# Two-layer decoder trunk on one core: smaller first loads kept to four in flight, a shorter warm-up, and a reordered last reduction and store

## The chip, the cores and the metric

The kernel runs on one core of a Trainium2 chip. The metric is the time of one execution on the device in microseconds (us). Three timed runs of the kernel before gave 958.12, 958.21 and 958.51 us, so the median is 958.21. A separate execution was recorded by the hardware profiler; its rows are what this document reads.

Engines are named as in the profile: PE is TensorE's matmuls, PEld its weight loads, DVE is VectorE, ACT is ScalarE, POOL is GpSimd and SP is SyncE. A q behind a name is the engine's instruction queue, which issues DMAs.

## What is computed

The input x is 256 positions by 2048 features, in float32. Two layers follow each other, and a last RMS norm ends the computation:

```python
def _rmsnorm(x, g):
    y = x32 * lax.rsqrt(jnp.mean(x32 * x32, axis=-1, keepdims=True) + NORM_EPS)
    return y * g
# layer 0: h = rmsnorm(x) @ w_in, cut into q, k, v of 8 dilated heads, q, k, v of 4 differential heads, gate z
#          y = concat(dilated mixture, differential attention) * silu(z);  x = x + y @ w_out
# layer 1: h = rmsnorm(x) @ w_in, cut into q, k, v of 16 causal heads, gate z
#          y = attention * silu(z);                                         x = x + y @ w_out
# out = rmsnorm(x, final_norm)
```

Each layer multiplies by 2048 x 8192 input weights and 2048 x 2048 output weights, in float32. So the two layers read 168 MB of weights.

## The kernel before

**Tiling.** The contraction of 2048 is cut into 16 k-tiles of 128. The output columns are cut into chunks: 512 columns wide for v and for the output projection, 256 for q, k and z. Layer 0 begins with a v chunk. In such a chunk each k-tile takes six matmuls of 512 columns, three for each half of the 256 positions.

**Splitting.** Every float32 operand is split into a high part, rounded to the fp32r type, and a low part, the rest. ScalarE makes the high part with a copy (lines 130 and 133), VectorE the low part with a subtraction (131 and 134). A product is then high x high, high x low and low x high (`mm3`, line 310). For x the copy also multiplies by the norm's weight g (`split_x`, lines 162 and 163).

**Loads.** One weight tile `raw` holds four k-tiles of a 512-wide chunk, 1 MB; three of them fit. `load(n)` fetches the tile and `split(m)` splits one half of it, two k-tiles. `split` runs three halves ahead of the matmuls. All loads go through SP's queue in the order in which they are written. The first four tiles (line 95 on) are cut: k-tile 0, k-tile 1, then two at a time, with an x piece of two k-tiles (256 KB) ahead. From tile 4 on a tile is one DMA (line 106).

**Start.** TensorE does ten 128 x 128 float32 matmuls on a constant tile of ones first (line 148; each appears as two passes in the profile). They feed nothing. ScalarE loads its function table meanwhile.

**End.** `last_chunk` does the last 512 columns of the output projection, first for positions 0 to 127, then for 128 to 255 in two pieces of 256 columns. Behind the last matmul VectorE adds the residual (line 471), ScalarE squares the result and accumulates (473), VectorE scales that and adds the sum of the earlier columns (478), GpSimd raises it to the power -0.5 (480). VectorE and ScalarE multiply the four 512-wide pieces by that factor in turn (486, 488), and SP stores them (489).

Of the kernel before, what the change touches and what calls it, by code (L numbers as in the profile page):

```python
# [2 lines left out]

# [5 lines left out]
F32 = mybir.dt.float32  # L9
F32R = mybir.dt.float32r  # L10
AF = mybir.ActivationFunctionType
ALU = mybir.AluOpType
# [3 lines left out]
P = 128  # L16
S = 256
D = 2048
KT = D // P
# [3 lines left out]
SCALE = HD ** -0.5  # L23
LAM_INIT = 0.8 - 0.6 * math.exp(-0.3 * 0)
AHEAD = 3
WARM = 10
RAW_BUFS = 3
SPLIT_BUFS = 4
ALIGN = 512
PAD = 160  # L30
BACK = 224
# [24 lines left out]
def trunk(ctx, tc, x_nat, x_t, w0, o0, w1, o1, g0, g1, gfin, lam, subln, cos_t, sin_t,  # L56
# [30 lines left out]
    def source(n):  # L87
        layer, i = divmod(n, n_layer)
        return (w0, w1)[layer][i] if i < n_in else (o0, o1)[layer][i - n_in]

    def load(n):
        if n >= NR or n in raws:
            return
        t = wpool.tile([P, 4 * CW], F32, tag="raw", name=f"raw{n}", bufs=RAW_BUFS)
        if n == 0:
            for i in range(3):
                if i != 1:
                    load_x(i)
                nc.sync.dma_start(t[:, (0, 1, 2)[i] * CW:(1, 2, 4)[i] * CW],  # L99
                                  source(0)[:, (0, 1, 2)[i] * CW:(1, 2, 4)[i] * CW])  # L100
        elif n < 4:
            for a in (0, 2):
                load_x(4 * n + a)
                nc.sync.dma_start(t[:, a * CW:(a + 2) * CW], source(n)[:, a * CW:(a + 2) * CW])
        else:
            nc.sync.dma_start(t, source(n))
        raws[n] = t
        for f in after_load.get(n, ()):
            f()

    def split(m):
        if m >= 2 * NR:
            return
        load(m // 2)
        r = raws[m // 2][:, 2 * (m % 2) * CW:2 * (m % 2 + 1) * CW]
        last = m - 2 * NR + 8
        if 0 <= last < 4:
            h = [xhl[2 * last + i].rearrange("p a b -> p (a b)") for i in range(2)]
            lo = [xhl[8 + 2 * last + i].rearrange("p a b -> p (a b)") for i in range(2)]
        else:  # L120
            ht = wpool.tile([P, 2 * CW], F32R, tag="wh", name=f"wh{m}")
            lt = wpool.tile([P, 2 * CW], F32R, tag="wl", name=f"wl{m}")
            w = wide[m // 2]
            h, lo = ([t[:, i:i + w] for i in range(0, 2 * CW, w)] for t in (ht, lt))
        if m < 2 or 0 <= last < 4:
            for i in range(2):
                if m == 0:
                    split_x(0, i, xr(i))
                rr = r[:, i * CW:(i + 1) * CW]
                nc.scalar.activation(h[i], rr, AF.Copy)  # L130
                nc.vector.tensor_sub(lo[i], rr, h[i].bitcast(F32))
        else:
            nc.scalar.activation(ht, r, AF.Copy)  # L133
            nc.vector.tensor_sub(lt, r, ht.bitcast(F32))  # L134
        splits[m] = (h, lo)
# [5 lines left out]
    nc.vector.memset(ones, 1.0)  # L141
    nc.vector.memset(half, -0.5)
    warm = small.tile([P, 1], F32, tag="warm", name="warm")
    nc.scalar.activation(warm, half, AF.Tanh)
    xraw = [work.tile([P, 4, S], F32, tag=f"yt{i}", name=f"xraw{i}") for i in range(KT // 4)]
    pw = patt.tile([P, P], F32, tag="O", name="pw")
    for i in range(WARM):
        nc.tensor.matmul(pw, ones, ones, start=True, stop=True)
    def load_x(kt):
        nc.sync.dma_start(xraw[kt // 4][:, kt % 4:kt % 4 + 2], x_t[:, kt:kt + 2])  # L150
        if kt == 0:
            nc.sync.dma_start(g_sb[:, 0], g0)

    def xr(kt):
        return xraw[kt // 4][:, kt % 4]
# [151 lines left out]
                nc.scalar.activation(v, ps[:, tt], AF.Copy, scale=rs)  # L307
        V[layer, g] = (v, vh, vl)

    def mm3(out_, lh, ll, rh, rl, start=True, stop=True):  # L310
        for i, (l, r) in enumerate(((lh, rh), (lh, rl), (ll, rh))):
            nc.tensor.matmul(out_, l, r, start=start and i == 0, stop=stop and i == 2)  # L312

    def softmax(layer, g, h, mask):
        (q, qh, ql), (k, kh, kl) = Q[layer, g], K[layer, g]
# [127 lines left out]
    def last_chunk():  # L443

        base = 2 * NR - 8
        part = small.tile([P, 2], F32, tag="part", name="part")
        fs = small.tile([P, 2, 4], F32, tag="fs", name="fs")
        c0 = 3 * CW
        for tt, widths in ((0, (CW,)), (1, (CW // 2, CW // 2))):
            nc.vector.memset(fs[:, tt], 0.0)  # L450
            at_col = 0
            for i, w in enumerate(widths):
                ps = pacc.tile([P, w], F32, tag="acc", name=f"last{tt}_{i}")
                for kt in range(KT):
                    if tt == 0 and kt % 2 == 0:
                        split(base + kt // 2 + AHEAD)
                    wh, wl = splits[base + kt // 2]
                    cs = slice(at_col, at_col + w)
                    a_h, a_l = yh[kt][:, tt * P:(tt + 1) * P], yl[kt][:, tt * P:(tt + 1) * P]
                    b_h, b_l = wh[kt % 2][:, cs], wl[kt % 2][:, cs]  # L460
                    for j, (l, r) in enumerate(((a_h, b_h), (a_h, b_l), (a_l, b_h))):
                        nc.tensor.matmul(ps, l, r, start=kt == 0 and j == 0, stop=kt == KT - 1 and j == 2)  # L462
                    if tt == 0:
                        for f, a in fill.pop(4 * NR - KT + kt, []):
                            f(*a)
                if i == 0:
                    s = small.tile([P, 1], F32, tag="s1", name="s1", bufs=2)
                    nc.vector.tensor_reduce(s, ssq[:, tt, 0:3], axis=AX.X, op=ALU.add)
                    nc.vector.tensor_scalar(part[:, tt:tt + 1], s, 1.0 / D, EPS, op0=ALU.mult, op1=ALU.add)
# [12 lines left out]
                at_col += w  # L482
            for n in range(4):
                x = x_sb[:, tt, n * CW:(n + 1) * CW]
                if n % 2 == 0:
                    nc.vector.tensor_scalar(x, x, fs[:, tt, 3:4], None, op0=ALU.mult)
                else:
                    nc.scalar.activation(x, x, AF.Copy, scale=fs[:, tt, 3:4])
                nc.sync.dma_start(out[tt * P:(tt + 1) * P, n * CW:(n + 1) * CW], x)


    at(14, first_r_a)
# [12 lines left out]
    for (kind, layer, g, j, w), slot0 in list(zip(chunks, starts))[:-1]:  # L505
# [3 lines left out]
        for slot in range(slot0, nxt):  # L509
            if slot % 2 == 0:  # L510
                split(slot // 2 + AHEAD)
                load((slot // 2 + AHEAD) // 2 + 1)
            if layer == 0 and slot < KT and 2 * AHEAD <= slot + 4 < KT:
                split_x(0, slot + 4, xr(slot + 4))
            wh, wl = splits[slot // 2]
            for i in range(per):
                kt = (slot - slot0) * per + i
                ww = (slot % 2) * per + i
                first, final = kt == 0, kt == KT - 1
                for b in range(2):  # L520
                    bs = slice(b * P, (b + 1) * P)
                    if w == CW:
                        a_h, a_l = (yh[kt][:, bs], yl[kt][:, bs]) if kind == "o" else \
                            (xhl[kt][:, 0, bs], xhl[kt][:, 1, bs])
                        mm3(ps[:, b], a_h, a_l, wh[ww], wl[ww], start=first, stop=final)
# [109 lines left out]
```

## Time and profile before

| | |
|---|---|
| timed runs, median of 3 | 958.21 us (958.12 to 958.51) |
| profiled execution | 958.89 us, of which its span is 957.1 us |
| TensorE busy | 946.3 us, 99% of the span |
| VectorE, ScalarE busy | 639.3 us (67%), 526.3 us (55%) |
| read from HBM, written | 174.15 MB, 2.10 MB |
| mean granted TensorE clock | 0.996 of full speed |

The span runs from the first instruction to the last. A busy share is an average over the whole span. A row of a timeline tells when an instruction started, how long it took and, in brackets, how long its engine had been idle and what ended that. The granted clock is a share of 2.4 GHz, so 0.50 is 1.2 GHz.

### The profile page before, as it was taken

The numbers are of one execution on the slowest core, as the hardware profiler recorded it, in microseconds if no ns is written. First come the engines' busy times: TensorE is split into PE (matmuls) and PEld (weight loads), VectorE is DVE, ScalarE is ACT, GpSimd is POOL, SyncE is SP. The second block draws the span as 40 slices with busy tenths as digits, with TensorE's granted clock in tenths as the row PEclk, the third lists the DMA queues.
The fourth block names the chain that finished last, engine by engine and source line by source line (L and its number), as shares of the span: only waits on it lengthen the run. The fifth ranks groups of instructions, "written<-read, shape, count | busy, mean of one in ns | idle before, by whom it ended". The sixth has DMA issues, their size and how long they took to land.

```text
span 957.1 us, 13108 instructions
## 1 busy us (share of the span) xinstructions
PE 946.3 (99%) x5132; PEld 819.1 (86%) x5132; DVE 639.3 (67%) x973; ACT 526.3 (55%) x807; POOL 6.0 (1%) x12
## 2 busy tenths in 40 slices
PE   8999999999999999999999999999999999999996
PEld 7888888888888888888888898888889888888886
DVE  6778678557856785655566787685678567755572
ACT  7556556445645564454544665564566455644451
POOL 0000000000000000000000000000000000000000
PEclk9999999999999999999999999999999999999999
DMA  9775454445554554544555544545454545554542
GB/s 327 247 295 181 146 190 176 169 175 195 185 173 162 196 179 175 176 176 176 181 176 203 190 169 156 203 155 194 164 191 170 182 173 180 191 205 176 181 171 88
DMA packets 27854, 177.09 MB, mean 185 GB/s; under 512 B 3344, under 2 KB 4112, under 8 KB 7696
## 3 DMA queue, kind: packets, MB, share of 16 engines
q1 hardware_dynamic: 27504, 175.21, 51.5%
q10 hardware_dynamic: 288, 1.05, 0.4%
q8 instruction: 40, 0.66, 0.3%
q14 instruction: 22, 0.18, 0.1%
HBM read 174.15 MB, written 2.10 MB: 184 GB/s over the span
## 4 chain that ended last, share of the span: by engine, by line
PE 96%; issue 1%; DMA 1%; SPq 0%; ACT 0%; DVE 0%; POOL 0%; POOLq 0%; ACTq 0%
PE acc L529 36%; PE acc L312 34%; PE acc L531 19%; PE ps_s L312 1%; PE last L462 1%; PE ps_t L352 1%; DMA raw<-in_w 1%; PE po L312 1%; PE ps_s L317 1%; PE po L383 1%; PE pdo L312 0%; PE ps_xt L426 0%; PE ps_yt L409 0%; SPq L99 0%; SPq L150 0%
## 5 line engine op out<-in xcount | busy, mean ns | idle before, releaser
L134 DVE TENSOR_TENSOR wl<-raw,wh 128x1024 fp32r<-128x1024 f32 x314 | 384.3, 1224 | 244.7 <-ACT wh L133 242.2
L529 PE MATMUL acc<-x,wh 128*128 128x512 f32 x1536 | 541.1, 393 | 0.0
L133 ACT ACTIVATE wh<-raw 128x1024 fp32r<-128x1024 f32 x314 | 332.3, 1059 | 292.5 <-PE acc L529 138.4
L531 PE MATMUL acc<-x,wl 128*128 128x256 f32 x1536 | 432.8, 282 | 0.0
L529 PEld LDWEIGHTS acc<-x,wh 128*128 128x128 f32 x1536 | 288.5, 188 | 58.4
L531 PEld LDWEIGHTS acc<-x,wl 128*128 128x128 f32 x1536 | 290.2, 189 | 0.3
L312 PE MATMUL acc<-wh,x 128*128 128x512 f32 x512 | 164.8, 400 | 1.6 <-ACT wh L130 1.6
L312 PEld LDWEIGHTS acc<-wh,x 128*128 128x128 f32 x512 | 96.9, 189 | 24.8 <-ACT wh L130 1.8
L312 PE MATMUL acc<-wl,x 128*128 128x512 f32 x256 | 101.9, 398 | 0.5 <-DVE wl L134 0.2
L312 PE MATMUL acc<-wh,yh 128*128 128x512 f32 x224 | 88.4, 394 | 0.0
L312 PE MATMUL acc<-wh,yl 128*128 128x512 f32 x224 | 87.3, 390 | 0.0
L312 PE MATMUL acc<-wl,yh 128*128 128x512 f32 x224 | 87.2, 389 | 0.0
L312 PEld LDWEIGHTS acc<-wl,x 128*128 128x128 f32 x256 | 48.5, 190 | 12.6 <-DVE wl L134 0.7
L312 PEld LDWEIGHTS acc<-wh,yl 128*128 128x128 f32 x224 | 42.0, 188 | 9.0
L312 PEld LDWEIGHTS acc<-wl,yh 128*128 128x128 f32 x224 | 42.1, 188 | 8.3
L312 PEld LDWEIGHTS acc<-wh,yh 128*128 128x128 f32 x224 | 42.1, 188 | 8.3
L326 ACT ACTIVATE p<-p,st 128x128 f32<-128x128 f32 x64 | 28.5, 448 | 9.9 <-DVE st L322 9.6
L375 ACT ACTIVATE yh<-y 128x256 fp32r<-128x256 f32 x32 | 13.0, 417 | 34.4 <-DVE y L374 34.3
L290 DVE TENSOR_TENSOR rt<-rt,sr 128x512 f32<-128x512 f32 x32 | 22.1, 690 | 3.7 <-ACT rt L288 2.4
L287 ACT ACTIVATE rt<-rt 64x512 f32<-64x512 f32 x32 | 20.2, 631 | 7.7 <-DVE rt L286 7.0
L286 DVE TENSOR_TENSOR rt<-acc,rt 128x512 f32<-128x512 f32 x32 | 21.8, 683 | 0.1
L288 ACT ACTIVATE rt<-rt 64x512 f32<-64x512 f32 x32 | 20.2, 632 | 0.4
(131 smaller groups left out, 646.9 us busy)
## 6 DMA issues: line engine op xcount, KB each, us to landing
raw<-in_w SPq DMA_DIRECT2D x124, 1024.0 KB, 4.7
raw<-in_o SPq DMA_DIRECT2D x32, 1024.0 KB, 4.7
raw<-in_w SPq DMA_DIRECT2D x7, 512.0 KB, 8.7
xraw<-in_x_t SPq DMA_DIRECT2D x8, 256.0 KB, 7.7
x_sb<-in_x_nat SPq DMA_DIRECT2D x1, 2048.0 KB, 11.0
out<-x_sb SPq DMA_DIRECT2D x8, 256.0 KB, 2.5
gf<-in_gfin ACTq DMA_DIRECT2D x2, 512.0 KB, 4.5
raw<-in_w SPq DMA_DIRECT2D x2, 256.0 KB, 4.5
```

Source lines behind the costliest of these rows:

```text
L133: nc.scalar.activation(ht, r, AF.Copy)
L134: nc.vector.tensor_sub(lt, r, ht.bitcast(F32))
L286: nc.vector.tensor_add(t1, ps[:, :, 0:S], t1)
L287: nc.scalar.activation(t2[0:64], t1[64:128], AF.Copy)
L288: nc.scalar.activation(t2[64:128], t1[0:64], AF.Copy)
L290: nc.vector.tensor_mul(t2, t2, sr[:, None, :].to_broadcast([P, 2, S]))
L312: nc.tensor.matmul(out_, l, r, start=start and i == 0, stop=stop and i == 2)
L317: nc.tensor.matmul(ps[:, 0:P], q[:, h, 0:P], k[:, h, 0:P], start=True, stop=True)
L326: nc.scalar.activation(p[:, sl], p[:, sl], AF.Exp, bias=st[:, 0, i:i + 1], scale=-1.0, accum_out=st[:, 1, i:i + 1])
L375: nc.scalar.activation(yh[kt], y, AF.Copy)
L529: nc.tensor.matmul(ps[:, b], wh[ww][:, bs], xx, start=first, stop=False, skip_group_check=True)
L531: nc.tensor.matmul(ps[:, b, 0:S], wl[ww][:, bs], xx[:, 0:S], start=False, stop=final, skip_group_check=True)
```

## The change

**Loads.** The first four weight tiles and the x pieces with them now go through `fetch`, which makes each load wait until the fourth one before it has landed. The pieces are smaller: k-tile 0 comes in two halves of its columns (128 KB each), k-tiles 1 to 7 one by one (256 KB), k-tiles 8 to 15 in twos as before. x comes as one k-tile (128 KB) with each single weight piece, as two with each double one. The norm's weight g and x of k-tile 0 move from SP's queue to ScalarE's, ahead of its table load.

**Splits and first matmuls.** The copies and subtractions of k-tiles 4 to 7 are done one k-tile at a time (before: two). Those of k-tile 0 are done in two halves of 256 columns, and so are its matmuls: twelve of 256 columns in place of six of 512. The warm-up has five matmuls in place of ten.

**End.** The square, its accumulation and the scaling become one VectorE instruction, a multiply with a running sum that starts at the part known before. The final piece's multiplication by the norm's weight and by the factor become one. The pieces stored are 256 to 512 columns wide and go through both queues: 256, 512, 512 (and for the last positions 256) from VectorE by SP, 256 and the rest from ScalarE by its own queue.

```diff
-WARM = 10
+WARM = 5
...
+IN_FLIGHT = 4
...
+    fetched = []
+
+    def fetch(dst, src):
+
+        i = nc.sync.dma_start(dst, src).ins
+        if len(fetched) >= IN_FLIGHT:
+            tc.add_manual_dep(i, fetched[-IN_FLIGHT].name, mybir.DependencyInfo(
+                mybir.DependencyClass.Sync, mybir.DependencyReason.DATA), reason="loads in turn")
+        fetched.append(i)
...
-        if n == 0:
-            for i in range(3):
-                if i != 1:
-                    load_x(i)
-                nc.sync.dma_start(t[:, (0, 1, 2)[i] * CW:(1, 2, 4)[i] * CW],
-                                  source(0)[:, (0, 1, 2)[i] * CW:(1, 2, 4)[i] * CW])
-        elif n < 4:
-            for a in (0, 2):
-                load_x(4 * n + a)
-                nc.sync.dma_start(t[:, a * CW:(a + 2) * CW], source(n)[:, a * CW:(a + 2) * CW])
+        if n < 4:
+
+            cuts = {0: (0, CW // 2, CW, 2 * CW, 3 * CW, 4 * CW), 1: range(0, 5 * CW, CW)}.get(n, range(0, 5 * CW, 2 * CW))
+            for a, b in zip(cuts, cuts[1:]):
+                if a % CW == 0 and (n or a):
+                    load_x(4 * n + a // CW, max(1, (b - a) // CW))
+                fetch(t[:, a:b], source(n)[:, a:b])
...
-        if m < 2 or 0 <= last < 4:
+        if m < 4 or 0 <= last < 4:
...
-                rr = r[:, i * CW:(i + 1) * CW]
-                nc.scalar.activation(h[i], rr, AF.Copy)
-                nc.vector.tensor_sub(lo[i], rr, h[i].bitcast(F32))
+                n = CW // 2 if m == 0 and i == 0 else CW
+                for a in range(0, CW, n):
+                    rr = r[:, i * CW + a:i * CW + a + n]
+                    nc.scalar.activation(h[i][:, a:a + n], rr, AF.Copy)
+                    nc.vector.tensor_sub(lo[i][:, a:a + n], rr, h[i][:, a:a + n].bitcast(F32))
...
+    nc.scalar.dma_start(g_sb[:, 0], g0)
+    nc.scalar.dma_start(xraw[0][:, 0:1], x_t[:, 0:1])
     nc.scalar.activation(warm, half, AF.Tanh)
...
-    def load_x(kt):
-        nc.sync.dma_start(xraw[kt // 4][:, kt % 4:kt % 4 + 2], x_t[:, kt:kt + 2])
-        if kt == 0:
-            nc.sync.dma_start(g_sb[:, 0], g0)
+    def load_x(kt, n):
+        fetch(xraw[kt // 4][:, kt % 4:kt % 4 + n], x_t[:, kt:kt + n])
...
-                nc.scalar.activation(j, x, AF.Square, accum_out=fs[:, tt, i:i + 1])
-                if i + 1 < len(widths):
-                    nc.vector.tensor_scalar(part[:, tt:tt + 1], fs[:, tt, i:i + 1], 1.0 / D, part[:, tt:tt + 1],
-                                            op0=ALU.mult, op1=ALU.add)
-                else:
-                    nc.vector.tensor_scalar(fs[:, tt, 2:3], fs[:, tt, i:i + 1], 1.0 / D, part[:, tt:tt + 1],
-                                            op0=ALU.mult, op1=ALU.add)
-                    nc.gpsimd.tensor_tensor(fs[:, tt, 3:4], fs[:, tt, 2:3], half, op=ALU.pow)
-                nc.vector.tensor_mul(x, x, gf[1][:, CW + at_col:CW + at_col + w])
+                mean = e5[:, tt, 3 + i:4 + i]
+                nc.vector.tensor_tensor_reduce(out=j, in0=x, in1=x, scale=1.0 / D, scalar=part, op0=ALU.mult,
+                                               op1=ALU.add, accum_out=mean)
+                part = mean
+                if i + 1 == len(widths):
+                    nc.gpsimd.tensor_tensor(rf, mean, half, op=ALU.pow)
+                if tt == 0 or i == 0:
+                    nc.vector.tensor_mul(x, x, gf[1][:, CW + at_col:CW + at_col + w])
...
-                nc.sync.dma_start(out[tt * P:(tt + 1) * P, n * CW:(n + 1) * CW], x)
+
+            last = () if tt == 0 else ((D - CW // 2, D),)
+            mid = D - CW // 2 * len(last)
+            pieces = ((0, 256), (256, 768), (768, 1280), *last), ((1280, 1536), (1536, mid))
...
+                    if c in last:
+                        nc.vector.scalar_tensor_tensor(x, x, rf, gf[1][:, 2 * CW - CW // 2:], op0=ALU.mult, op1=ALU.mult)
+                    elif e == 0:
+                        nc.vector.tensor_scalar(x, x, rf, None, op0=ALU.mult)
+                    else:
+                        nc.scalar.activation(x, x, AF.Copy, scale=rf)
+                    (nc.sync, nc.scalar)[e].dma_start(out[tt * P:(tt + 1) * P, c[0]:c[1]], x)
...
-                for b in range(2):
+
+                halves = ((0, CW // 2), (CW // 2, CW)) if slot == 0 else ((0, CW),)
+                for (c0, c1), b in ((c, b) for c in halves for b in range(2)):

```

SP's queue at the start of the program, before; `xraw` is x, `raw` a weight tile, `g_sb` the norm's weight.

```order
L150 DMA xraw_101<-in_x_t 128x512
L152 DMA g_sb<-in_g 128x16
L99 DMA raw_124<-in_w 128x512 x2
L150 DMA xraw_101<-in_x_t 128x512
L99 DMA raw_124<-in_w 128x1024
L150 DMA xraw_102<-in_x_t 128x512
L104 DMA raw_151<-in_w 128x1024
L150 DMA xraw_102<-in_x_t 128x512
```

And the same place now.

```order
L97 DMA raw_121<-in_w 128x256 x2
L97 DMA xraw_100<-in_x_t 128x256
L97 DMA raw_121<-in_w 128x512
L97 DMA xraw_100<-in_x_t 128x256
L97 DMA raw_121<-in_w 128x512
L97 DMA xraw_100<-in_x_t 128x256
L97 DMA raw_121<-in_w 128x512
L97 DMA xraw_101<-in_x_t 128x256
L97 DMA raw_152<-in_w 128x512
L97 DMA xraw_101<-in_x_t 128x256
```

The queue now starts with the two halves of weight tile 0, x alternates with single k-tiles of weights, and g is gone from it. Every row from the fifth load on also waits for the load four before it, which the rows do not print.

ScalarE at the start of the program, before; `x` is the high part of an x tile, `wh` the high part of a weight tile.

```order
L144 ACT_TABLE_LOAD
L144 ACTIVATE warm<-half 128x1
L162 ACTIVATE x_59<-xraw_101,g_sb 128x256
L162 ACTIVATE x_60<-xraw_101,g_sb 128x256
L130 ACTIVATE wh_131<-raw_124 128x512 x2
L162 ACTIVATE x_61<-xraw_101,g_sb 128x256
L162 ACTIVATE x_62<-xraw_101,g_sb 128x256
L130 ACTIVATE wh_141<-raw_124 128x512 x2
```

And now.

```order
L156 DMA g_sb<-in_g 128x16
L157 DMA xraw_100<-in_x_t 128x256
L158 ACT_TABLE_LOAD
L158 ACTIVATE warm<-half 128x1
L141 ACTIVATE wh_130<-raw_121 128x256
L173 ACTIVATE x_59<-xraw_100,g_sb 128x256
L141 ACTIVATE wh_130<-raw_121 128x256
L173 ACTIVATE x_60<-xraw_100,g_sb 128x256
L141 ACTIVATE wh_130<-raw_121 128x512
L173 ACTIVATE x_61<-xraw_100,g_sb 128x256
L141 ACTIVATE wh_142<-raw_121 128x512
L173 ACTIVATE x_62<-xraw_100,g_sb 128x256
```

Two DMA issues stand ahead of the table load, a half weight copy stands ahead of the first x copy, and copies of single k-tiles of x and weights alternate.

VectorE at the end of the program, before; `fs` holds sums and the factor, `gf` the last norm's weight.

```order
L481 TENSOR_TENSOR x_sb<-x_sb,gf_7838 128x256
L471 TENSOR_TENSOR x_sb<-last_1_8311,x_sb 128x256
L478 TENSOR_SCALAR fs<-fs,part 128x1
L481 TENSOR_TENSOR x_sb<-x_sb,gf_7838 128x256
L486 TENSOR_SCALAR x_sb<-x_sb,fs 128x512 x2
```

And now; `e` holds sums and the factor, the two ISA rows are the reduction and the reading of its sum.

```order
L481 TENSOR_TENSOR x_sb<-last_1_8321,x_sb 128x256
L484 ISA junk_l,e_8175<-x_sb,e_8175 128x256
L484 ISA e_8175 128x1
L504 TENSOR_SCALAR x_sb<-x_sb,e_8175 128x256
L504 TENSOR_SCALAR x_sb<-x_sb,e_8175 128x512 x2
L502 SCALAR_TENSOR_TENSOR x_sb<-x_sb,e_8175,gf_7853 128x256
```

The reduction stands right behind the add, and the last multiplication by `gf` moves to the last row, joined with the factor.

## Rows read from the trace of the kernel before

**Rows 1.** Stretches: us, busy us (instructions) of TensorE, granted clock, DMA share, GB/s.

```profile
2.00:6.70 4.70, 3.09 (x18) 1.00 0.82 238
7.70:11.00 3.30, 3.30 (x9) 0.50 0.99 333
11.20:15.08 3.88, 3.63 (x16) 1.00 1.04 413
6.70:15.08 8.38, 7.90 (x25) 0.80 1.02 370
15.08:31.91 16.83, 16.83 (x72) 1.00 0.94 344
31.91:949.40 917.49, 917.49 (x5017) 1.00 0.51 181
```

**Rows 2.** Order of time, first 16 us: start, us, engine, line, instruction, [idle before <- releaser].

```profile
0.73 1.28 ACT L144 ACT_TABLE_LOAD   x1 [0.73 <-PEq L625]
0.74 0.38 SPq L150 DMA_DIRECT2D xraw<-in_x_t  x1
...
3.78 0.91 ACT L162 ACTIVATE x<-xraw,g_sb 128x256 fp32r<-128x256 f32 x2 [1.55 <-DMA g_sb<-in_g]
...
6.02 1.32 ACT L130 ACTIVATE wh<-raw 128x512 fp32r<-128x512 f32 x2 [1.33 <-DMA raw<-in_w]
...
6.70 0.49 PE L312 MATMUL acc<-wh,x 128*128 128x512 f32 x1 [1.62 <-ACT wh L130]
...
7.43 0.57 PE L312 MATMUL acc<-wl,x 128*128 128x512 f32 x1 [0.23 <-DVE wl L131]
...
15.08 0.50 PE L312 MATMUL acc<-wl,x 128*128 128x512 f32 x1 [0.25 <-DVE wl L134]
```

**Rows 3.** Order of time, the end; same columns.

```profile
939.93 0.93 POOL L480 TENSOR_TENSOR fs<-fs,half 128x1 f32<-128x1 f32 x1 [455.84 <-DVE fs L478]
...
949.48 0.42 DVE L471 TENSOR_TENSOR x_sb<-last,x_sb 128x256 f32<-128x256 f32 x1 [4.09 <-PE last L462]
950.00 0.42 ACT L473 ACTIVATE junk_l<-x_sb 128x256 f32<-128x256 f32 x1 [5.19 <-DVE x_sb L471]
...
950.54 0.21 DVE L478 TENSOR_SCALAR fs<-fs,part 128x1 f32<-128x1 f32 x1 [0.64 <-ACT junk_l L473]
...
950.84 0.66 POOL L480 TENSOR_TENSOR fs<-fs,half 128x1 f32<-128x1 f32 x1 [9.97 <-DVE fs L478]
...
951.53 0.88 DVE L486 TENSOR_SCALAR x_sb<-x_sb,fs 128x512 f32<-128x512 f32 x2 [0.45 <-POOL fs L480]
```

**Rows 4.** The head of the page.

```profile
span 957.1 us, 13108 instructions
```

**Rows 5.** The stores of line 489 (duration ns min/median/max); the DMA engines while data flows.

```profile
L489 SPq DMA_DIRECT2D out<-x_sb x8: 332/406/450, 941.6 to 953.5; - x8
...
952.80:955.60 2.80, 0.57 0.97 375
```

**Rows 6.** Loads issued before 30 us: count, KB each, median us to landing.

```profile
raw<-in_w SPq DMA_DIRECT2D x7, 512.0 KB, 8.7
...
raw<-in_w SPq DMA_DIRECT2D x2, 256.0 KB, 4.5
```

**Rows 7.** Stretches of the warm-up, its passes alone (columns as in group 1, PEld added).

```profile
3.00:4.00 1.00, 1.00 (x7) 1.00 (x7) 1.00 0.86 214
4.40:5.10 0.70, 0.69 (x7) 0.49 (x5) 1.00 1.00 260
```

**Rows 8.** Groups by line and shape, first 30 us: busy us, mean ns, idle before.

```profile
L134 DVE TENSOR_TENSOR wl<-raw,wh 128x1024 fp32r<-128x1024 f32 x8 | 9.7, 1222 | 2.1 <-ACT wh L133 2.1
L133 ACT ACTIVATE wh<-raw 128x1024 fp32r<-128x1024 f32 x9 | 9.4, 1056 | 1.0 <-DMA raw<-in_w 0.6 <-PE acc L312 0.3
```

**Rows 9.** Groups by line and shape, 800 to 832 us: busy us, mean ns, idle before.

```profile
L322 DVE CUSTOM_DVE_ANT_0 p<-ps_s,mc 128x256 f32<-128x256 f32 x4 | 1.7, 420 | 0.0
...
L322 DVE DVE_READ_ACCUMULATOR2_ANT st<- 128x1 f32 x8 | 0.7, 83 | 0.0
```

More of the change, by code (lines that the diff above doesn't have):

```diff
@@ L2 @@
 from contextlib import ExitStack
+from itertools import zip_longest
 import concourse.bass as bass
@@ L143, in trunk @@
     warm = small.tile([P, 1], F32, tag="warm", name="warm")
+    xraw = [work.tile([P, 4, S], F32, tag=f"yt{i}", name=f"xraw{i}") for i in range(KT // 4)]
+    nc.scalar.dma_start(g_sb[:, 0], g0)
+    nc.scalar.dma_start(xraw[0][:, 0:1], x_t[:, 0:1])
     nc.scalar.activation(warm, half, AF.Tanh)
-    xraw = [work.tile([P, 4, S], F32, tag=f"yt{i}", name=f"xraw{i}") for i in range(KT // 4)]
     pw = patt.tile([P, P], F32, tag="O", name="pw")
@@ L308, in evac_v, with mm3 @@
         V[layer, g] = (v, vh, vl)
-    def mm3(out_, lh, ll, rh, rl, start=True, stop=True):
+    def mm3(out_, lh, ll, rh, rl, start=True, stop=True, **kw):
         for i, (l, r) in enumerate(((lh, rh), (lh, rl), (ll, rh))):
-            nc.tensor.matmul(out_, l, r, start=start and i == 0, stop=stop and i == 2)
+            nc.tensor.matmul(out_, l, r, start=start and i == 0, stop=stop and i == 2, **kw)
     def softmax(layer, g, h, mask):
@@ L445, in last_chunk @@
         base = 2 * NR - 8
-        part = small.tile([P, 2], F32, tag="part", name="part")
-        fs = small.tile([P, 2, 4], F32, tag="fs", name="fs")
         c0 = 3 * CW
+        e5 = small.tile([P, 2, 5], F32, name="e5")
         for tt, widths in ((0, (CW,)), (1, (CW // 2, CW // 2))):
-            nc.vector.memset(fs[:, tt], 0.0)
+            rf, s, part = (e5[:, tt, i:i + 1] for i in range(3))
             at_col = 0
@@ L466, in last_chunk @@
                 if i == 0:
-                    s = small.tile([P, 1], F32, tag="s1", name="s1", bufs=2)
                     nc.vector.tensor_reduce(s, ssq[:, tt, 0:3], axis=AX.X, op=ALU.add)
-                    nc.vector.tensor_scalar(part[:, tt:tt + 1], s, 1.0 / D, EPS, op0=ALU.mult, op1=ALU.add)
+                    nc.vector.tensor_scalar(part, s, 1.0 / D, EPS, op0=ALU.mult, op1=ALU.add)
                 x = x_sb[:, tt, c0 + at_col:c0 + at_col + w]
@@ L481, in last_chunk @@
-                nc.vector.tensor_mul(x, x, gf[1][:, CW + at_col:CW + at_col + w])
-                at_col += w
[L483 to L488, printed above, removed]
-                nc.sync.dma_start(out[tt * P:(tt + 1) * P, n * CW:(n + 1) * CW], x)
+                mean = e5[:, tt, 3 + i:4 + i]
@@ new lines, in last_chunk @@
+            mid = D - CW // 2 * len(last)
+            pieces = ((0, 256), (256, 768), (768, 1280), *last), ((1280, 1536), (1536, mid))
+            for pair in zip_longest(*pieces):
+                for e, c in enumerate(pair):
+                    if c is None:
+                        continue
+                    x = x_sb[:, tt, c[0]:c[1]]
+                    if c in last:
[5 more added lines that the diff above has]
+                    (nc.sync, nc.scalar)[e].dma_start(out[tt * P:(tt + 1) * P, c[0]:c[1]], x)
@@ L524, in trunk @@
                             (xhl[kt][:, 0, bs], xhl[kt][:, 1, bs])
-                        mm3(ps[:, b], a_h, a_l, wh[ww], wl[ww], start=first, stop=final)
+                        mm3(ps[:, b, c0:c1], a_h, a_l, wh[ww][:, c0:c1], wl[ww][:, c0:c1],
+                            start=first and c0 == 0, stop=final, skip_group_check=slot0 == 0)
                     else:
```

## The prediction, made before the change was run

> **What bounds the kernel now.** The table of busy time by stretch comes first, because it says where there is anything to win. From 31.91 to 949.40 us TensorE is busy for the whole 917.49 us, at the full granted clock [rows 1], while the 16 DMA engines are half used. Nothing that only frees ScalarE, VectorE or a queue can shorten that stretch, and the change leaves its matmuls as they are. What is left are the two ends: everything before TensorE's stream becomes unbroken at 15.08 us [rows 2], and the 7.65 us from the last matmul (949.45, where the row of 949.48 finds it done [rows 3]) to the end of the span at 957.1 [rows 4].
>
> The start is read from the rows in order of time. The first x tiles are copied by ScalarE at 3.78, but the first weight tile is there only at 6.02 (that row's wait is on the load), and the first matmul starts at 6.70 [rows 2]. From there to 15.08 come 25 matmuls in 8.38 us; afterwards 72 take 16.83 us, 0.234 us each [rows 1]. At that pace the 25 need 5.84 us. So the whole kernel runs as if an unbroken full-speed stream had begun at 15.08 − 5.84 = 9.24 us. I call this the zero point; whatever the change does to the start is its shift of the zero point. Of the 2.54 us between 6.70 and 9.24 about 1.7 are the clock: from 7.7 to 11.0 the granted clock is 0.50, the 1.2 GHz level [rows 1]. The rest are two waits, 0.73 us from the first matmul to the second for VectorE's subtraction, and the last break before 15.08, for a 128x1024 subtraction [rows 2].
>
> The end is one chain: add on VectorE 949.48, Square with accumulation on ScalarE 950.00, scalar step on VectorE 950.54, power on GpSimd 950.84, and the factor is there at 951.53 [rows 3]. Then four 256 KB stores; data flows in 952.8 to 955.6 with the DMA engines at 0.97 of their time [rows 5].
>
> **The first matmul.** Now ScalarE's queue issues g and the 128 KB x tile 0 first. An issue takes about 0.38 us [rows 2], so x leaves at about 1.2, and the table load (1.28 us [rows 2]) ends near 3.0 instead of 2.0, still before the data. Before, x and g issued by 1.2 were usable at 3.78, about 2.6 us after the last issue. That gives x at 3.8, its copy 0.45 us (half of the 0.91 for two), and a first matmul at 4.3 to 4.4. The weights' first half, 128 KB, is the first thing on SP's queue and is copied ahead of x. The bound above: if it needs 4.5 us like the 256 KB loads of before [rows 6], it lands at 5.2, and half a copy and x's copy later the matmul starts near 6.1. Below nothing: a first matmul later than 6.70 would need a load longer than any of that size. I take 4.4.
>
> **The clock after it.** The warm-up is cut from 10 matmuls to 5, of two passes each, so it ends near 3.1 instead of 5.1. Its pace shows that it began slow: seven passes in 1.00 us at 3 to 4, seven in 0.70 us after 4.4 [rows 7]. Before, TensorE sped up during the warm-up, idled from 5.1 to 6.7, was slowed at 7.7 and came back shortly after 11.0, after dense matmuls at half speed [rows 1]. Cut short, the warm-up probably ends before the fast level. Then the real matmuls begin at 1.2 GHz and lose half of the time that they run there. The one slow stretch that the rows show cost 3.4/2 = 1.7 us; I take the same, for work that is as dense. Bounds: 0 (five matmuls suffice) and (11.1 − 4.4)/2 = 3.35 (slow until the moment at which it ended before). By the clock the zero point is 4.4 + 1.7 = 6.1.
>
> The Trainium skill speaks against this edit: "TensorE: Matmul & The Clock Gate", section "Part 1", has the slow level as the default state that only sustained work releases, and says that the watching does not restart with the kernel, so the moment of a rise varies from run to run. By it the loss is not a constant that one profile tells; a long slow stretch is the third rival below. The rows of before agree with the first half (slow passes first, fast ones later); one profile cannot show the second.
>
> **The supply.** At full speed TensorE eats a k-tile, 384 KB of weights and x, in 6 x 0.234 = 1.40 us. Loads now wait for the fourth one before them, and the pieces are 128 and 256 KB up to k-tile 7, then 256 and 512 KB. The chain that matters is every fourth load: second half of weight tile 0 (issued about 1.2), tile 2, tile 4, tile 6, then the 512 KB of tiles 8 and 9, behind which stand the first 1024-wide copy and subtraction, 1.06 + 1.22 us [rows 8]. The second matmul of k-tile 8 is the 50th, so its zero point is that time less 49 x 0.234 = 11.46. Loads of 256 KB took 4.5 us when everything was queued, and 512 KB 8.7 [rows 6]; limited to 768 KB in flight, at the 238 to 333 GB/s of the start [rows 1], a round is 2.3 to 3.2 us. I take 2.8 for four rounds and 3.6 for the 512 KB: landing at 1.2 + 11.2 + 3.6 = 16.0, operands at 18.3, zero point 6.84. From below: everything through k-tile 9 is 3.84 MB plus g; at the rates of before (1.12 MB by 6.7, 1.4 more by 11.0, the rest at 413 GB/s [rows 1]) it is there at 14.2, zero point 5.0. From above, five rounds of 4.5: landing 23.7, zero point 14.5. The value is taken near the low end because the 4.5 us was measured behind other loads in a queue that was kept full. Behind a load that waits on SP stand all later loads, and ScalarE's copies and then TensorE wait for those.
>
> The Trainium skill has a rule against this part too: "DMA: Bandwidth & Descriptors", section "Rules for kernel authors", wants transfers of 1 MiB and more for full bandwidth. In the rows, loads of 256 and 512 KB in a full queue ran at 413 GB/s, more than the 344 of the stretch in which the 1 MB loads begin [rows 1], so size alone costs nothing here; whether it does with four in flight, no row shows. By the rule rivals 2 and 4 are the likelier ones; by the row the sum stands.
>
> Clock and supply thus give zero points of 6.1 and 6.84; the two losses overlap, since a slow TensorE needs less, and the later one counts: 6.84, the start gains 9.24 − 6.84 = **2.4 us**. The split of the first k-tile's six matmuls into twelve of 256 columns, and of the copies of tiles 4 to 7, costs only fixed overhead: a few times 0.1 us, on ScalarE and VectorE beside loads. The small reordering near the first evacuation stays in the stretch where TensorE never waits.
>
> **The end.** The Square on ScalarE, its accumulator read and the VectorE step become one VectorE reduction right behind the add: a 128x256 one takes 420 ns and its read 83 [rows 9]. Add done at 949.90, so the power starts near 950.40 to 950.45 instead of 950.84: 0.4 us. The next piece is 256 columns instead of 512 and goes to the store about 0.15 us earlier. Bounds: 0.9 if the shorter last store also ends earlier by its 0.33 us of data, 0.2 if this power takes 0.93 us, as the one at 939.93 did, instead of 0.66 [rows 3]. The stores then flow at the rate of before. Two of them now leave from ScalarE, where an issue holds up its next piece by some 0.4 us; with 0.97 of the DMA time used, and 256 KB taking 0.7 us at 375 GB/s against issues of 0.33 to 0.45 us [rows 5], neither that nor the second queue changes when the last byte is out. I take **0.5 us**.
>
> **Sum.** 2.4 + 0.5 = 2.9 us. The profiled execution took 958.89 (span 957.1 and 1.8 around it), 0.7 more than the median of the timed runs, 958.21; the shift is applied to the median: 955.3 us.
>
> **Rivals.**
> 1. Supply as good as the lowest bound and the clock high early: zero point 5.2, gain 4.0 + 0.6, 953.6. For: fewer loads at once may also shorten the first ones, whose DMA engines were only 0.82 busy before 6.7 [rows 1]. Against: those rates are then reached with far less queued.
> 2. Loads in turn starve TensorE a little: rounds of 3.3 us and 4.1 for the last put the zero point at 1.2 + 13.2 + 4.1 + 2.3 − 11.46 = 9.3. The start gains nothing, the end 0.5: 957.7. For: two k-tiles take TensorE 2.81 us, so any round above that accumulates. Against: half speed at the start gives slack.
> 3. The slow clock lasts until 11.1: zero point 4.4 + 3.35 = 7.75, gain 1.5 + 0.5, 956.2. For: the shorter warm-up. Against: dense work from 4.4 on.
> 4. Slower: the same limit of four loads, rounds of 4.0 and 4.8. Zero point 12.8, 3.6 us lost, 0.5 won: 961.3. It decides from rounds of about 3.75 on; for it stands the 4.5 us of before [rows 6], against it that those loads stood in a full queue.
>
> **How the numbers follow.** Forecast 0.55 (its own range 954.4 to 956.2), rivals 0.17, 0.13, 0.10, 0.05. A change under about 0.2%, 1.9 us, can't be told from none by a measurement of this kernel; the line is at 956.3. Faster: forecast, rival 1 and a little over half of rival 3, 0.78. Same: rival 2 and the rest, 0.17. Slower 0.05. The range leaves out rival 4 and the outer edges of 1 and 2: 953.6 to 957.5.
>
> **What would show it.** First real matmul between 4.1 and 4.8; a granted clock of 0.50 from there to between 6.9 and 9; TensorE unbroken from about k-tile 9 on, with the waits before it on the 128x1024 subtraction of tiles 8 and 9; power on GpSimd about 0.95 us after the last matmul instead of 1.39. The prediction is wrong if TensorE waits for loads after k-tile 10, if anything breaks the stream between 32 us and the end, or if the first matmul is not before 5.5.

## The result

The changed kernel took 963.99 us (median of four runs, 961.26 to 964.30), the kernel before 958.34 beside it (958.12 to 958.51). The ratio is 1.0053, with a 95% interval of 1.0034 to 1.0071: 5.6 us slower, where 955.3 was predicted and 957.5 was the top of the range. The profiled execution is the fastest of the four, 961.26 us; its span is 2.3 us longer than that of [rows 4]. One execution of the kernel before beside these experiments (1917 us) and one of a variant (1345 us) were far off and are left out of the ratios below.

```profile
span 959.4 us, 13117 instructions
```

Stretches of the changed kernel, in the columns of [rows 1] with PEld, VectorE, ScalarE and GpSimd between TensorE and the clock.

```profile
4.40:7.70 3.30, 2.90 (x13) 2.88 (x14) 2.40 (x5) 2.84 (x7) 0.00 (x0) 1.00 0.82 264
7.70:11.00 3.30, 3.30 (x11) 2.60 (x11) 2.17 (x4) 1.80 (x4) 0.00 (x0) 1.00 0.78 240
11.00:15.00 4.00, 4.00 (x19) 3.22 (x18) 2.79 (x6) 2.72 (x6) 0.00 (x0) 1.00 0.76 251
15.00:20.00 5.00, 3.63 (x16) 2.60 (x14) 1.96 (x5) 1.71 (x4) 0.00 (x0) 1.00 0.84 269
20.00:25.00 5.00, 3.29 (x13) 2.48 (x14) 3.94 (x6) 3.56 (x6) 0.00 (x0) 1.00 0.98 302
25.00:46.00 21.00, 20.68 (x107) 17.17 (x105) 17.45 (x22) 14.78 (x17) 0.70 (x1) 1.00 0.87 318
46.00:47.00 1.00, 0.78 (x4) 0.69 (x5) 0.89 (x3) 1.00 (x3) 0.00 (x0) 1.00 0.93 353
47.00:952.00 905.00, 905.00 (x4944) 784.86 (x4942) 606.73 (x922) 493.25 (x757) 4.51 (x6) 1.00 0.51 180
```

Read the last two columns first. From 7.7 to 15 the DMA engines are 0.76 to 0.78 busy at 240 to 251 GB/s, where before they were full at 333 and 413 [rows 1]. Then TensorE, busy to 15, loses 1.37 us up to 20 and 1.71 up to 25. A smaller loss lies between 25 and 47; after that nothing is lost. What TensorE waited for, from 6 to 60 us (total, times, longest):

```profile
PE acc L323 <- ACT wh L144: 2.3, 1, 2.3
PE acc L323 <- DVE wl L145: 0.8, 1, 0.8
PE acc L550 <- ACT v L318: 0.5, 1, 0.5
```

The chain of work that leads to these waits, in order of time (start, us, what):

```profile
1.17 2.72 DMA raw<-in_w
...
3.91 3.12 DMA raw<-in_w
...
7.05 3.54 DMA raw<-in_w
...
10.61 3.09 DMA raw<-in_w
...
13.72 6.02 DMA raw<-in_w
...
19.84 1.06 ACT wh L144
...
20.93 1.24 DVE wl L145
...
22.21 1.90 PE acc L323 x7
```

These are the loads that the supply step named: each is issued when the one before it in the chain has landed. The row at 22.21 starts with the 50th matmul, the second of k-tile 8. Its zero point is 22.21 − 11.46 = 10.75, against 9.24 before: the start lost 1.51 us.

The first matmul came nearly as forecast (start, us, instruction, idle before):

```profile
4.24 0.51 ACT L173 ACTIVATE x<-xraw,g_sb 128x256 fp32r<-128x256 f32 x1 [0.64 <-DMA xraw<-in_x_t]
...
4.80 0.58 PE L323 MATMUL acc<-wh,x 128*128 128x256 f32 x1 [1.25 <-ACT x L173]
```

The first matmul starts 1.9 us earlier than in [rows 2], behind the x tile. It starts slow, as a second look at TensorE alone shows:

```profile
8.47 1.05 PE L323 MATMUL acc<-wh,x 128*128 128x512 f32 x2
9.32 0.63 PE L323 MATMUL acc<-wl,x 128*128 128x512 f32 x1
...
10.54 0.63 PE L323 MATMUL acc<-wh,x 128*128 128x512 f32 x2
11.00 0.40 PE L323 MATMUL acc<-wl,x 128*128 128x512 f32 x1
```

Two matmuls take 0.85 us at 8.47 and 0.46 at 10.54, so the pace doubles near 10. The clock column of the stretches prints 1.00 for 7.7 to 11.0 all the same, so the pace has to be read instead. Slow from 4.80 to about 9.9 means a loss of some 2.5 us.

The second loss is at the first evacuation of v. ScalarE there, before the change and then after it:

```profile
40.59 0.69 ACT L303 ACTIVATE vh<-acc,rn 128x512 fp32r<-128x512 f32 x1 [2.15 <-POOL rn L201]
41.17 1.05 ACT L133 ACTIVATE wh<-raw 128x1024 fp32r<-128x1024 f32 x1
42.12 0.68 ACT L307 ACTIVATE v<-acc,rn 128x512 f32<-128x512 f32 x1
```

```profile
42.47 1.06 ACT L144 ACTIVATE wh<-raw 128x1024 fp32r<-128x1024 f32 x1 [2.49 <-PE acc L550]
43.43 0.67 ACT L314 ACTIVATE vh<-acc,rn 128x512 fp32r<-128x512 f32 x1
45.48 0.69 ACT L318 ACTIVATE v<-acc,rn 128x512 f32<-128x512 f32 x1 [1.38 <-DVE vl L315]
```

The weight copy now stands ahead of `vh`, and on VectorE the subtraction of 1.23 us (43.56) stands between `vh` and `vl` (44.70). `v` comes at 45.48 and frees the accumulator late; the next chunk's matmul that needs it starts at 46.22:

```profile
45.26 0.39 PE L550 MATMUL acc<-x,wh 128*128 128x512 f32 x1
...
46.22 0.50 PE L550 MATMUL acc<-x,wh 128*128 128x512 f32 x1 [0.45 <-ACT v L318]
```

From one L550 matmul to the next are 0.96 us here, 0.35 elsewhere in this stretch: 0.61 us lost, 0.45 of it idle. Four one-column matmuls for the sum of squares hold the stream at 40.56 by 0.33 us more than their like did at 38.34 before; a second trace of this same program (below) lacks these 0.33 us, so they are not the change's. The last add starts 2.59 us later than in [rows 3]: 1.51 by the zero point, 0.61 and 0.33 here, and 0.14 that stay unexplained.

The end:

```profile
952.07 0.42 DVE L481 TENSOR_TENSOR x_sb<-last,x_sb 128x256 f32<-128x256 f32 x1 [4.29 <-PE last L472]
952.53 0.48 DVE L484 CUSTOM_DVE_ANT_0 junk_l<-x_sb,e 128x256 f32<-128x256 f32 x1
952.94 0.08 DVE L484 DVE_READ_ACCUMULATOR2_ANT e<- 128x1 f32 x1
953.10 0.55 POOL L488 TENSOR_TENSOR e<-e,half 128x1 f32<-128x1 f32 x1 [9.79 <-DVE e L484]
953.68 0.91 ACT L506 ACTIVATE x_sb<-x_sb,e 128x256 f32<-128x256 f32 x2 [8.68 <-POOL e L488]
```

From the add to the factor's first use are 1.61 us, 2.05 in [rows 3]; from there to the end of the span 5.72 against 5.57. So the chain gained 0.44 and the stores gave 0.15 back: 0.29 in all. 2.59 − 0.29 is the 2.3 us of the span.

### The profile page after: what moved, and what is told of

Same layout as the page of the kernel before. It is cut to its first block, busy times and chain, and to the rows that moved or that the text cites. A ratio compares the mean times of both kernels' runs of the same rounds, so it can differ in the third digit from the quotient of the medians.

```text
span 959.4 us, 13117 instructions
## 1 busy us (share of the span) xinstructions
PE 946.1 (99%) x5128; PEld 818.7 (85%) x5128; DVE 641.4 (67%) x979; ACT 524.6 (55%) x804; POOL 6.0 (1%) x12
## 4 chain that ended last, share of the span: by engine, by line
PE 95%; DMA 2%; issue 1%; DVE 1%; ACT 0%; POOL 0%; POOLq 0%; DVEq 0%; SPq 0%; ACTq 0%
PE acc L550 36%; PE acc L323 33%; PE acc L552 19%; DMA raw<-in_w 2%; PE ps_s L323 1%; PE last L472 1%; PE ps_t L363 1%; PE po L323 1%; PE ps_s L328 1%; PE po L394 1%; PE pdo L323 0%; PE ps_xt L437 0%; ACT wh L144 0%; DVE wl L145 0%; PE ps_yt L420 0%
## 5 line engine op out<-in xcount | busy, mean ns | idle before, releaser
L550 PE MATMUL acc<-x,wh 128*128 128x512 f32 x1536 | 541.3, 393 | 0.5 <-ACT v L318 0.5
L550 PEld LDWEIGHTS acc<-x,wh 128*128 128x128 f32 x1536 | 288.5, 188 | 59.1 <-ACT v L318 0.8
L323 PE MATMUL acc<-wh,x 128*128 128x512 f32 (+1 forms) x516 | 165.9, 399 | 3.6 <-ACT wh L144 2.3
L323 PE MATMUL acc<-wl,x 128*128 128x512 f32 (+1 forms) x258 | 102.6, 398 | 0.8 <-DVE wl L145 0.8
```

## The experiments

Two theories stood at first. One: the limit of four small loads leaves the DMA engines too little to work on. The other: small pieces are slow by themselves. Times are medians beside the kernel before on the same chip: 958.48 for the repeat, no limit, the limit of eight and the new end alone; 958.42 for the two with k-tiles 8 to 15 one by one; 958.31 for the rest.

**The changed kernel once more.**

> The changed kernel as it is, a second time. Its four runs so far gave 961.3 once and 963.8 to 964.3 three times, and the trace at hand is that of 961.3. If a stretch at the slow clock after the wait for k-tile 8 makes the difference, a trace near 964 shows a granted clock of 0.50 again after 20 us and some 2.5 us lost there; if the loads make it, the 512 KB load of k-tiles 8 and 9 lands later than the 19.74 us of the trace at hand.

962.22 us, ratio 1.0041 (1.0026 to 1.0056). The 512 KB land at 19.96, and the waits at k-tile 8 are 2.7 and 0.8 us. Afterwards, in this run, the clock fell:

```profile
23.05:26.45 3.40, 3.40 (x10) 2.66 (x9) 2.92 (x5) 2.73 (x6) 0.00 (x0) 0.50 1.03 330
```

3.4 us at 0.50, the 1.2 GHz level, with TensorE busy throughout: 1.7 us more lost, and none of it is in a list of waits. In the first profile, with waits of 2.3 and 0.8, the clock stayed at 1.00. The Trainium skill ("TensorE: Matmul & The Clock Gate", section "Part 1") has the slow level come back after idling. One of these two traces agrees, the other shows no fall, and no run here shows what decides between them.

The span of this trace is accounted for. The 50th matmul stands at 22.44, zero point 10.98, so the start lost 1.74 us; the slow stretch took 1.7 and the evacuation 0.61, the end gave 0.29 back: 3.8 us, and the span is 960.9, 3.8 more than [rows 4]. The one-column matmuls cost no more here than before (0.79 us from 42.33, as from 38.34 before). The four first runs list mean clocks of 0.998 (961.26) and 0.994 (the three of 963.76 to 964.30), so a longer slow stretch is the likely reason for their spread, but this is not shown.

**The limit taken away, and the limit at eight.**

```diff
-IN_FLIGHT = 4
+IN_FLIGHT = 100     # first run
+IN_FLIGHT = 8       # second run
```

> The changed kernel without the wait of a load for the fourth one before it (limit 100, never reached); pieces, queues, warm-up and end as changed. Theory 1 (the limit of four starves the DMA engines, which are busy 0.76 to 0.82 of the time from 7.7 to 15 us where before it was 0.99 to 1.04): the DMA engines go back to about 1.0, the 2.3 us wait ahead of k-tile 8 goes, and the time falls by 3 to 6 us to 956 to 960. Theory 2 (small pieces are slow, limit or not): the DMA share stays near 0.8 and the time within 1 us of the changed kernel's.

> The changed kernel with eight loads in flight in place of four. Theory 1: most of the gain of having no limit, 956 to 960; if the first loads profit from a limit, it is the faster of the two. Theory 2: no change, 961 to 964.

957.91 and 957.92 us, ratio 0.9996 (0.9987 to 1.0006) for both: four us come back, with the small pieces kept. With eight in flight the stretch from 7.7 to 11 reads

```profile
7.70:11.00 3.30, 3.30 (x16) 2.67 (x16) 3.30 (x8) 3.27 (x7) 0.00 (x0) 1.00 1.04 368
```

where four gave 0.78 and 240. The two longest loads of the chain, at the limit of eight:

```profile
4.98 4.47 DMA raw<-in_w
...
9.47 6.29 DMA raw<-in_w
```

The 512 KB of k-tile 8 take 6.29 us, not less than the 6.02 under the limit of four; they are only issued 4.25 us earlier. The waits at k-tile 8 shrink to 0.3 us.

**The limit on the old pieces.** The kernel before, its loads sent through the same `fetch`.

```diff
+IN_FLIGHT = 4
...
-                nc.sync.dma_start(t[:, a * CW:(a + 2) * CW], source(n)[:, a * CW:(a + 2) * CW])
+                fetch(t[:, a * CW:(a + 2) * CW], source(n)[:, a * CW:(a + 2) * CW])
```

> The kernel before with the limit of four loads alone: its own pieces (x 256 KB, weights 256 and 512 KB), its order, warm-up and end. Theory 1 (what the limit costs is bytes in flight: four small loads are too few): four of these pieces are 1.0 to 1.5 MB, as much as the limit of eight held, so the DMA engines stay above 0.9 busy and the time is that of before within 1 us, or better by up to 1 us since the first weight tile no longer shares with eight loads behind it. Theory 2 (waiting for landings on SP's queue costs by itself, whatever the size): slower than before by 2 us or more.

958.14 us, ratio 0.9995 (0.9986 to 1.0005). Four loads in flight cost nothing when they are of 256 and 512 KB:

```profile
7.70:11.00 3.30, 3.30 (x10) 2.63 (x9) 2.82 (x6) 2.55 (x6) 0.00 (x0) 1.00 0.96 338
```

So neither the number four nor the small piece is slow by itself; the two together are. Bytes in flight over the time to land should give the rate. Changed kernel: 2 x (256 + 128) KB in 3.2 us, the median of its 256 KB loads, 246 GB/s. Limit of eight: twice that in 4.3 us, 366. Old pieces, four: 2 x (512 + 256) KB in 4.7, 335. The rows above print 240, 368 and 338. TensorE at full speed wants 393 KB per 1.40 us, 280 GB/s. These sums describe each rate with a landing time that was measured beside it; they do not forecast the landing time.

**The limit only through k-tile 7.**

```diff
-        if len(fetched) >= IN_FLIGHT:
+        if IN_FLIGHT <= len(fetched) < 16:
```

> The changed kernel with the limit of four for k-tiles 0 to 7 only (its first 16 loads); the loads of k-tiles 8 to 15 don't wait for landings. In the trace of the changed kernel the load of k-tiles 8 and 9 is issued at 13.72 when k-tile 6 lands and takes 6.0 us, and SP then stands until 19.80. If the slow rounds up to k-tile 7 make the loss, k-tiles 8 and 9 are issued about 1.5 us sooner at best and 2 of the 4 to 5 us against the limit of eight come back (959.5 to 961). If the last round makes it, nearly all comes back: 958 to 959.

961.15 us, ratio 1.0033 (1.0020 to 1.0046). No load from k-tile 8 on waits, and yet most of the loss stays: the 512 KB go out at 13.16, only 0.6 us earlier than under the limit throughout, and take 6.79 us. TensorE waits 2.5 and 0.8 us there, and its clock is at 0.50 from 22.60 to 26.01. From 11 us on the stretches read

```profile
11.00:15.00 4.00, 4.00 (x18) 3.19 (x17) 2.95 (x6) 2.39 (x5) 0.00 (x0) 1.00 0.75 233
15.00:20.00 5.00, 3.46 (x14) 2.17 (x12) 1.76 (x4) 1.54 (x3) 0.00 (x0) 1.00 0.88 284
```

though six loads, 2.3 MB, were issued from 12.68 to 15.11. So bytes in flight do not set the rate alone: behind the slow rounds it stayed low for some 5 us more, and what was not fetched by 13 us was not made up in time. Why is not shown.

**K-tiles 8 to 15 one by one too**, with the limit as changed, and with the limit through k-tile 7. The question was whether the loss belongs to the step from one-tile to two-tile pieces.

```diff
-            cuts = {...4 * CW), 1: range(0, 5 * CW, CW)}.get(n, range(0, 5 * CW, 2 * CW))
+            cuts = {...4 * CW)}.get(n, range(0, 5 * CW, CW))
...
-        if m < 4 or 0 <= last < 4:
+        if m < 8 or 0 <= last < 4:
```

> The limit of four stays; k-tiles 8 to 15 are loaded and split one by one too (256 KB of weights and 128 KB of x each). Theory 1a (the loss comes where pieces of one k-tile are followed by one of two: 512 KB that take 6.0 us, of which nothing can be used before all has landed): the weights of k-tile 8 land 3 to 3.6 us after their issue at about 13.7, so at 17.0 instead of 19.74; the wait of 2.3 + 0.8 us there falls below 0.6 and there is no second slow stretch; later k-tiles may each come a little late, since a round of 3.3 us brings two k-tiles, 1.65 us each against TensorE's 1.40; 958 to 960. Theory 1b (four small loads in flight starve the DMA engines, and k-tile 8 only happens to be where the reserve is used up): the rate stays at 240 to 270 GB/s, TensorE waits in several places between k-tile 8 and 16 by 3 us or more together, and the load of the next whole tile, issued late behind the last of these, adds a wait; 962 to 966.

964.90 us, ratio 1.0069 (1.0057 to 1.0081), the slowest of all. Its waits:

```profile
PE acc L550 <- ACT wh L144: 1.6, 1, 1.6
PE acc L552 <- DVE wl L145: 1.0, 1, 1.0
PE acc L323 <- ACT wh L141: 0.7, 2, 0.5
PE acc L323 <- DVE wl L142: 0.7, 3, 0.2
```

No wait at k-tiles 8 and 9 is over 0.3 us, as the theory of the step said; the loss came back behind k-tile 15, at the first whole tile of 1 MB (the upper two rows), and it brought a slow stretch with it (35 to 60 us: clock 0.93). The late piece is where the reserve runs out, not what uses it up.

> The limit of four holds only for the loads through k-tile 7, as in the run that was made with that alone (961.15 us, waits of 2.5 and 0.8 us at k-tile 8, whose 512 KB took 6.79 us); k-tiles 8 to 15 are loaded and split one by one. Theory 1a (the size of the piece at the hand-over): k-tile 8 lands within 4.3 us of its issue at about 13.2, so at 17.5 or before; wait there below 0.6 us, no second slow stretch, 957.5 to 959. Theory 1b (the late issue and the thin queue before it): the bytes ahead of k-tile 8 are the same, it lands little earlier than half of the 512 KB would, and the waits are spread over k-tiles 8 to 12 instead of gone; 960 to 962.

959.98 us, ratio 1.0020 (1.0011 to 1.0029): between the two expectations. Waits of 0.9 and 0.2 us at k-tiles 8 to 15, then 0.8 and 1.0 at the first whole tile. Against the limit through k-tile 7 with double pieces the median is 1.2 us lower, but the two ran on different chips and their intervals overlap, so that gain is not shown. What is shown is that the waits move: less at k-tile 8, more at the first whole tile.

**A longer warm-up** on top of the limit of eight.

```diff
-WARM = 5
+WARM = 10
```

> The changed kernel with a limit of eight and the warm-up of before, ten matmuls. If the short warm-up costs a slow stretch (granted clock risen at 7.75 with five), the clock is high from before the first real matmul or falls again as it did before at 7.7; in the first case 957.9 of the limit of eight falls by up to 1.3 us, in the second it rises by 1 to 2 us. If the loads decide and not the clock, it stays within 0.5 us of 957.9, since k-tile 8 waits for its load anyway.

957.80 us, ratio 0.9991 (0.9981 to 1.0001), no different from 957.92. TensorE does run fast from the first k-tile on,

```profile
5.51 0.40 PE L323 MATMUL acc<-wh,x 128*128 128x256 f32 x2
5.74 0.28 PE L323 MATMUL acc<-wl,x 128*128 128x256 f32 x1
```

(two matmuls in 0.23 us; the changed kernel took 0.43 for such a pair, at 6.12), but then it waits 2.7 us up to 60 us, 0.5 of them at the evacuation and the rest for loads and their splits. So the earlier fast clock shows no gain in the timed runs. This trace, of the slowest of the ten executions (959.15), also shows that eight loads in flight don't always move 368 GB/s:

```profile
7.70:11.00 3.30, 3.30 (x14) 2.62 (x15) 2.44 (x5) 2.12 (x4) 0.00 (x0) 1.00 0.96 286
```

Its 256 KB loads took 5.5 us in the median, 4.3 in the trace with five warm-up matmuls. Whether the warm-up or chance does that, no run here shows.

**The new end alone**, on the kernel before.

```diff
-                nc.scalar.activation(j, x, AF.Square, accum_out=fs[:, tt, i:i + 1])
+                nc.vector.tensor_tensor_reduce(out=j, in0=x, in1=x, scale=1.0 / D, scalar=part, op0=ALU.mult,
+                                               op1=ALU.add, accum_out=mean)
...
-                nc.sync.dma_start(out[tt * P:(tt + 1) * P, n * CW:(n + 1) * CW], x)
+                    (nc.sync, nc.scalar)[e].dma_start(out[tt * P:(tt + 1) * P, c[0]:c[1]], x)
```

> The kernel before with the changed last chunk alone. From the two traces the end went from 7.62 to 7.33 us after the last add's start, so 0.3 us faster than before, 957.9 to 958.2; the prediction's 0.5 us would be 957.7. If the new end costs something earlier, the time is above 958.5.

958.19 us, ratio 0.9998 (0.9989 to 1.0008): the time can't tell it from nothing. In its trace the last add starts at 950.02 and the span ends at 957.4, 7.38 us against 7.62 before: 0.24 us, which agrees with the 0.29 above.

**The evacuation's order** put back, on top of the limit of eight. `evac_ins` holds the copy to `vh` and the subtraction to `vl` of the first evacuation.

```diff
-            nc.scalar.activation(ht, r, AF.Copy)
-            nc.vector.tensor_sub(lt, r, ht.bitcast(F32))
+            with tc.issue_after(evac_ins[0]) if m == 14 else nullcontext():
+                nc.scalar.activation(ht, r, AF.Copy)
+            with tc.issue_after(evac_ins[1]) if m == 14 else nullcontext():
+                nc.vector.tensor_sub(lt, r, ht.bitcast(F32))
```

> The changed kernel with a limit of eight and the split of the 15th half tile held behind the first evacuation of v on ScalarE and VectorE, the order that the kernel before has there. In the traces with the changed order TensorE loses 0.6 us at that place (its matmul waits for line 318); with the order of before it loses nothing: 957.9 less 0.6 is 957.3. If the wait has another cause, it stays at 957.9.

956.86 us, ratio 0.9984 (0.9975 to 0.9994). This is the only version here whose interval lies below 1, so it is faster than the kernel before, by 0.16%. From 35 to 60 us the limit of eight without and with this order:

```profile
35.00:60.00 25.00, 24.54 (x143) 21.54 (x142) 18.08 (x26) 14.70 (x19) 0.70 (x1) 1.00 0.89 320
```

```profile
35.00:60.00 25.00, 25.00 (x147) 22.17 (x146) 19.00 (x26) 14.99 (x19) 0.70 (x1) 1.00 0.82 313
```

0.46 us of idle time are gone from TensorE, and with them the 0.61 us from start to start. The ratio moved by 0.0012, 1.1 us, but the two ran on different chips and their intervals overlap, so the 0.61 of the traces is the safer size.

All kernels together, by what the DMA engines had moved in the first 20 us of the profiled execution:

| kernel | MB by 20 us | ratio to before |
|---|---|---|
| changed, all single pieces | 4.45 | 1.0069 |
| changed, again | 4.63 | 1.0041 |
| changed | 4.66 | 1.0053 |
| limit through k-tile 7 | 4.72 | 1.0033 |
| the same, single pieces | 4.84 | 1.0020 |
| limit of eight, ten warm-up matmuls | 5.48 | 0.9991 |
| old pieces, limit of four | 5.88 | 0.9995 |
| no limit | 6.00 | 0.9996 |
| new end alone | 6.25 | 0.9998 |
| limit of eight | 6.26 | 0.9996 |
| limit of eight, evacuation's order | 6.26 | 0.9984 |
| before | 6.32 | 1 |

The two ends of that table as the trace prints them, the changed kernel with single pieces and the kernel before:

```profile
DMA packets 3589, 4.45 MB, mean 223 GB/s; under 512 B 527, under 2 KB 2311, under 8 KB 3589
```

```profile
DMA packets 2567, 6.32 MB, mean 316 GB/s; under 512 B 407, under 2 KB 407, under 8 KB 2550
```

Every version up to 4.84 MB is slower than the kernel before, none from 5.48 on is, and from there the ratio no longer follows the bytes. Between the two lies no version.

## Why the prediction was wrong

**The step that failed is the supply.** "I take 2.8 for four rounds and 3.6 for the 512 KB". The rounds were 2.72, 3.12, 3.54 and 3.09, 12.5 us in place of 11.2, and the 512 KB took 6.02 in place of 3.6: landing 19.74 instead of 16.0. So the last load makes 2.4 of these 3.7 us and the rounds 1.3. The rounds were reckoned with rates from stretches in which the queue was full, applied to 768 KB in flight; 2.8 is the middle of the 2.3 to 3.2 us that they give, and the slow end, 238 GB/s, was the right one. The 3.6 of the last load rests on no row: [rows 6] has 8.7 us in a full queue, and in six other traces here the first such load took 6.2 to 6.8. With less in the queue each load is quicker (3.2 us instead of 4.5 for 256 KB), but not in proportion, so the rate falls.

Rival 4 named the mechanism, but its time of 961.3 meets that of the profiled execution by luck. It put the rounds at 4.0, from 3.75 on to decide, and they were 3.1, nearer to the 3.3 of rival 2; its start lost 3.6 us where this one lost 1.51. The rest of the measured 961.26 came from the evacuation, from parts of the stream that no rival had, and from a profile before that was itself 0.7 above its median.

Between the two profiled executions the span was to fall by 2.9 us and rose by 2.3. Of these 5.2 us 3.9 are the supply (zero point 10.75 instead of 6.84), 0.6 the evacuation, 0.2 the end, and 0.5 the one-column matmuls and the unexplained rest. The median of the timed runs lies another 2.7 us above the profiled execution. A slow stretch such as that of the second trace is the likely reason; the three slower runs have no profile that could show it.

That the supply decides the start is shown by taking the limit away or doubling it. In the trace of the last run, with eight loads in flight and the evacuation's order, the 50th matmul stands at 18.30, zero point 6.84, the forecast's own number. The last add stands at 947.08, 2.40 us before that of [rows 3]: the whole shift of the zero point arrives at the end, as the prediction reckoned. That the numbers meet is partly luck, since the landing was made up of other pieces. Its span is 954.4, 2.7 us below [rows 4], but the timed medians of the two kernels differ by only 1.45 us.

**The rule weighed beside it.** "DMA: Bandwidth & Descriptors" of the Trainium skill, section "Rules for kernel authors", asks for 1 MiB and more per transfer. Small pieces ran at 368 GB/s with eight in flight, more than the old ones at the same place before, 333 [rows 1] (286 in the trace with the longer warm-up, whose time was no longer); so the size of a transfer alone did not decide here. The rule pointed to the right rivals for a reason that the runs do not bear out.

**The reordering near the first evacuation** was costed at nothing, because TensorE never waits there in [rows 1]. It cost 0.61 us, and nothing once the order was put back. So the prediction's own sign of being wrong, a break in the stream between 32 us and the end, came at 46.22. That TensorE was never idle says that its suppliers were in time, not by how much.

**The clock.** Some 2.5 us were lost instead of 1.7, inside the bounds; the slow level lasted to about 9.9, not to between 6.9 and 9. It gives a zero point of about 7.3, which the supply covers. A second slow stretch of 3.4 us behind the waits was not in the sum, and in one of two profiles of the changed kernel it added 1.7 us.

**The first matmul** was right at the edge, 4.80 within 4.1 to 4.8 where 4.4 was taken, behind x as reckoned. **The end** gained 0.24 to 0.29 where 0.5 was taken, within the bounds of 0.2 to 0.9: the chain gave its 0.44, and the smaller first store gave nothing; the stores ended 0.15 later.

## What to carry to other kernels

A limit on loads in flight is a limit on bytes in flight: divide the bytes by the time that one load takes to land, measured with that many in flight, and compare with what the consumer eats. That is an estimate and not a law: with eight in flight one trace moved 368 GB/s and another 286. When pieces are cut smaller, the count has to rise with them. And where the stream of the busiest engine never breaks, look up how late its suppliers could be before calling a reordering free.

## What was not expected of the hardware

With 768 KB in flight the DMA engines moved 240 to 251 GB/s and were still 0.76 to 0.78 busy by their own share, where eight small loads gave 368 GB/s and 1.04. So the share fell by a quarter and the rate by a third. After waits of 2.7 and 0.8 us TensorE ran at 0.50 of its clock for 3.4 us while fully busy; after 2.3 and 0.8 in another execution of the same program it did not. Such a stretch came in two more traces: with the limit through k-tile 7 (waits of 2.5 and 0.8) and with single pieces throughout (1.6 and 1.0).

It stays open why 512 KB take 6.0 to 6.8 us behind pieces of one k-tile, at a limit of four, of eight or of none, and a median of 4.7 where four loads of the old sizes are in flight. It also stays open why the rate stayed low between 13 and 18 us once the limit had ended at k-tile 7.
